# Twenty short streams of unread float32r matmuls, their two sides at other distances in SBUF, between the memory stage and layer 0 of an encoder trunk

## The chip, the cores and the metric

The kernel runs on one core of a Trainium2 chip. The metric is the device time of one launch, in microseconds (us), lower being better. A core has five engines with queues of their own: TensorE (matrix products, PE in the profile; its weight loads have a row of their own, PEld), VectorE (DVE), ScalarE (ACT), GpSimd (POOL) and SyncE (SP, which issues most of the DMAs).

## The reference

Two layers of a bidirectional encoder. `x` and the memory `mem` are 256 x 2048 float32. Each layer projects the normalised `x` onto 7,168 columns, which three head groups share, and projects their joined outputs back onto 2,048 columns.

```python
for l in range(DEPTH):                                   # DEPTH = 2
    h = rmsnorm(x, norm_g[l])
    proj = h @ w_in[l]                                   # 2048 x 7168
    a_x, a_b, a_c, a_g, d_q, d_k, d_v, d_g, m_q, m_g = jnp.split(proj, offsets, axis=-1)
    y_a = short_gated_conv(a_x, a_b, a_c, conv_w[l], conv_b[l]) * jax.nn.silu(a_g)
    ...                                                  # q, k = rmsnorm(d_q), rmsnorm(d_k); lam from lambda_*
    o_d = diff_attention(q, k, v, lam, slopes)           # softmax 1 minus lam times softmax 2, with ALiBi
    y_d = rmsnorm(o_d, diff_head_norm_g[l]) * (1.0 - lam_init) * jax.nn.silu(d_g)
    mkv = rmsnorm(mem, mem_norm_g[l]) @ w_mem_kv[l]      # 2048 x 1024
    ...                                                  # mk, mv, mq from mkv and m_q
    y_m = memory_attention(mq, mk, mv) * jax.nn.silu(m_g)
    x = x + jnp.concatenate([y_a, y_d, y_m], axis=-1) @ w_out[l]   # 2048 x 2048
```

## The kernel before, in words

**Products in three passes.** Every large product is made of float32r matmuls. Each operand is held as a rounded part `hi` and a remainder `lo`; `block` computes hi·hi, hi·lo and lo·hi for each 128 rows of the contraction and each of the two row tiles of `x` (the three lines of `products`, L320, L321 and L322 in the profile). The stationary side is a 128 x 128 piece of the transposed activations, the moving side a 128 x 512 piece of the weights. The activations lie in tiles of the pool `big` (`memT` for the memory, `xT` for the layer's input, `yT` for its output), of the shape [128, 2, 16, 256]: part (hi or lo), contraction tile, row. The pool has two buffers, so `yT` of layer 0 takes the one that `memT` leaves.

**Weights.** `load_w` loads two contraction tiles of 512 columns by DMA into `raw` (four buffers); ScalarE rounds them into `hi` (L294), VectorE subtracts to get `lo` (L295). `hi` and `lo` have four buffers each, so these two engines may run four loads ahead of TensorE and then wait for it.

**Stages.** The memory stage comes first: `memT` is built from `mem` by transposes, and keys and values of the memory are computed for both layers (two blocks of products for each layer). Layer 0 follows with 14 blocks of the input projection, the attention scores and their products in between, and four blocks of the output projection; then layer 1, the same.

**Order.** The tile framework schedules all instructions by a simulated time line, save those that are wrapped in `tc.keep_in_program_order`; these keep the order in which they are written among themselves. Before the change the matmuls of `warm`, small transposes and a number of instructions on ScalarE, VectorE and the DMA queues are wrapped so; the products of `block` are not. Score matmuls write to the pool `ps_s` (tag "s"), two PSUM banks; `block` accumulates in `ps_acc`, four banks.

Of the kernel before, what the change touches and what calls it, by code (L numbers as in the profile page):

```python
# [10 lines left out]
F32 = mybir.dt.float32  # L11
# [7 lines left out]
P = 128  # L19
# [13 lines left out]
NB = 512  # L33
# [14 lines left out]
def encoder(ctx: ExitStack, tc: tile.TileContext, x, mem, norm_g, w_in, conv_w, conv_b,  # L48
            dq_g, dk_g, lq1, lk1, lq2, lk2, head_g, mem_norm_g, w_mem_kv, mq_g, mk_g, w_out, out):
    nc = tc.nc  # L50
    x, mem, out = x[0], mem[0], out[0]

    def pool(name, bufs, space=None):
        kw = {"space": space} if space is not None else {}
        return ctx.enter_context(tc.tile_pool(name=name, bufs=bufs, **kw))
# [9 lines left out]
    ps_s = pool("ps_s", 2, PSUM)  # L65
# [4 lines left out]
    def nm(s):  # L70
        uid[0] += 1
        return f"{s}_{uid[0]}"
# [59 lines left out]
    def g_mnorm(l, k):  # L132
        return cva[:, l * KT + k:l * KT + k + 1]
# [74 lines left out]
    def later(g, n):  # L208
        due[id(g)] = chunk[0] + n
        return g  # L210
# [167 lines left out]
    def col(st, which, t):  # L378
        return st[:, which, t:t + 1]
# [23 lines left out]
    def normed(acc, gs, st, home):  # L403
        return normed_steps(nc.vector, acc, gs, st, home)
# [13 lines left out]
    def sheets(tag):  # L418
        return lambda: sheet(tmp if tag == "e" else keep, tag)
# [257 lines left out]
    def stats_of(parts, tag):  # L677
        ss = small.tile([P, NT], F32, tag="ssum", name=nm("ssum"))
        nc.vector.tensor_reduce(ss, parts, AX.X, ALU.add)
        return row_stats(ss, tag)  # L680

    def T_tile(what):
        kept.append(big.tile([P, 2, KT, SEQ], F32R, tag="T", name=nm(what)))
        return kept[-1]
# [9 lines left out]
    memT = T_tile("memT")  # L694
# [59 lines left out]
    def keys(l, nat):  # L754


        d = dram.tile([NA, B, NA, W_MEM // P * NT * B], F32, name=nm("kd"))
        flat = nat.rearrange("p b j t c -> p b (j t c)")
        for a in range(NA):
            tc.keep_in_program_order(nc.gpsimd.dma_start(d[:, :, a].rearrange("b c r -> c b r"), flat[a * B:(a + 1) * B]))  # L760
        tc.keep_in_program_order(nc.gpsimd.dma_start(flat, d.rearrange("b c a r -> (b c) a r")))
        yield 8
        tc.keep_in_program_order(nc.vector.transpose(
            mkT[l].rearrange("p j (t a i) -> p (j t) a i", t=NT, a=NA),
            nat.rearrange("p a j t c -> p (j t) a c")))
        yield
        tc.keep_in_program_order(nc.scalar.activation(mkT[l], mkT[l], AF.Copy, scale=mgain[:, l:l + 1]))
# [14 lines left out]
    for l in range(DEPTH):  # L782
        if l == 0:
            xT = T_tile("xT")
        mkT.append(keep.tile([P, MH, SEQ], F32, tag=f"mkT{l}", name=f"mkT{l}"))

        mv.append(keep.tile([P, NT, W_MEM], F32, tag="mv" if l == 0 else "bgx", name=f"mv{l}"))
        gm = lambda k: g_mnorm(l, k)
        pinned[0] = l == 0
        acc_k = block(memT, w_mem_kv[l], [(0, NB)], ALLK, gain=gm, before=mem_piece if l == 0 else x_load)  # L790
        if l == 0:
            kraw = keep.tile([P, NT, NB], F32, tag="ga", name="kraw")
            stm.append(keep.tile([P, 6, NT], F32, tag="stm", name="stm"))
        if l > 0:
            tasks.append(later(keys(l, normed(acc_k, P, stm[0], sheets("mqT"))), 10))
        acc = block(memT, w_mem_kv[l], [(W_MEM, NB)], ALLK, gain=gm, before=mem_norm if l == 0 else x_squares)
        pinned[0] = False
        acc_v.append(acc)
        if l > 0:
            for t in range(NT):  # L800
                nc.scalar.activation(mv[l][:, t, :], acc[t], AF.Copy, scale=col(stm[0], R, t))
            away.append(dram.tile([P, NT, W_MEM], F32, name=nm("mvd")))
            nc.sync.dma_start(away[-1], mv[l])
    for l in range(DEPTH):
        st = stats_of(ssx, "st")
        if l > 0:
# [16 lines left out]
        for b in order:  # L823
# [7 lines left out]
            if b == 4:  # L831
                start = chunk[0]
# [119 lines left out]
        for b in range(4):  # L952
# [3 lines left out]
            for t in range(NT):  # L956
                n = 256 if final else NB
# [41 lines left out]
```

## Time and profile before

| what | value |
|---|---|
| time, median of 2 runs | 929.75 us (929.09 and 930.41) |
| span of the profiled execution, first to last instruction | 926.6 us |
| matmul instructions | 4,170, each with a weight load |
| TensorE busy | 919.1 us (99%) |
| VectorE, ScalarE, GpSimd busy | 670.3, 498.7, 16.3 us |
| granted TensorE clock | 0.999 |
| DMA traffic | 215.05 MB, mean 232 GB/s |

The profile gives the span of the profiled execution; its own launch time is not listed apart from it. The median of the runs is 929.75 - 926.6 = 3.15 us longer than the span, which is what lies ahead of the first and behind the last instruction, give or take the spread of the runs. A matmul's row gives its start and its duration; matmuls are pipelined, so that the next one starts before the last has ended, and what one costs is the distance from start to start.

### The profile page before, as it was taken

How to read it: one execution, taken by the hardware profiler on the slowest of the kernel's cores; microseconds unless marked ns; L12 is line 12 of the kernel's file. 1: busy time of each engine (PE TensorE's matmuls, PEld its weight loads, DVE VectorE, ACT ScalarE, POOL GpSimd, SP SyncE). 2: the span in 40 equal slices, each digit the busy share in tenths (PEclk: the TensorE clock that was granted, in tenths of full speed). 3: DMA queues.
4: the chain of work that ended last, by engine and by line, in shares of the span. 5: the costliest groups of instructions: out<-in, count | busy, mean ns of one | idle time of the engine just before them, and what ended most of it. 6: DMA issues, size and time to landing. Idle time of an engine off the chain costs nothing.

```text
span 926.6 us, 12301 instructions
## 1 busy us (share of the span) xinstructions
PE 919.1 (99%) x4170; PEld 760.8 (82%) x4170; DVE 670.3 (72%) x1206; ACT 498.7 (54%) x779; POOL 16.3 (2%) x34
## 2 busy tenths in 40 slices
PE   9999999999999999999999999999999999999998
PEld 6878788888888888888888888888888888888886
DVE  5679788858798786467667757878898777558652
ACT  6758555575555554435455544568554554445431
POOL 0202100000000000000000000000000000000000
PEclk9999999999999999999999999999999999999999
DMA  7897868776669988978587766885889889988662
GB/s 251 251 306 242 304 216 236 234 224 193 191 205 240 254 258 233 269 244 256 205 270 246 235 197 213 246 232 175 249 228 226 258 214 253 252 235 240 210 218 74
DMA packets 251138, 215.05 MB, mean 232 GB/s; under 512 B 131182, under 2 KB 174020, under 8 KB 251076
## 3 DMA queue, kind: packets, MB, share of 16 engines
q1 hardware_dynamic: 248292, 208.76, 76.4%
q0 software_dynamic: 1440, 4.20, 1.6%
q10 hardware_dynamic: 1344, 1.33, 0.5%
q8 instruction: 32, 0.52, 0.2%
q14 instruction: 30, 0.25, 0.1%
HBM read 193.26 MB, written 20.97 MB: 231 GB/s over the span
## 4 chain that ended last, share of the span: by engine, by line
PE 90%; DVE 4%; ACT 3%; DMA 2%; issue 1%; ACTq 0%; DVEq 0%
PE acc L321 29%; PE acc L322 29%; PE acc L320 29%; DMA raw<-in_w_mem_kv_dram 2%; DVE lo L299 2%; PE po L470 2%; ACT hi L298 2%; DVE xf L662 1%; PE s L623 1%; PE s L578 1%; PE s L577 1%; ACT msq L716 0%; DVE xT L267 0%; DVE memT L264 0%; ACT memT L263 0%
## 5 line engine op out<-in xcount | busy, mean ns | idle before, releaser
L294 ACT CAST hi<-raw 128x1024 fp32r<-128x1024 f32 x288 | 302.7, 1052 | 349.8 <-PE acc L322 288.2
L295 DVE TENSOR_TENSOR lo<-raw,hi 128x1024 fp32r<-128x1024 f32 x288 | 351.8, 1223 | 188.4 <-ACT hi L294 178.4
L320 PE MATMUL acc<-hi,xT 128*128 128x512 f32 x896 | 350.5, 393 | 0.0
L322 PE MATMUL acc<-hi,xT 128*128 128x512 f32 x896 | 349.0, 390 | 0.0
L321 PE MATMUL acc<-lo,xT 128*128 128x512 f32 x896 | 348.9, 389 | 0.0
L322 PEld LDWEIGHTS acc<-hi,xT 128*128 128x128 f32 x896 | 168.2, 188 | 35.3
L321 PEld LDWEIGHTS acc<-lo,xT 128*128 128x128 f32 x896 | 168.4, 188 | 33.9
L320 PEld LDWEIGHTS acc<-hi,xT 128*128 128x128 f32 x896 | 168.2, 188 | 33.9
L320 PE MATMUL acc<-hi,yT 128*128 128x512 f32 x256 | 99.6, 389 | 0.0
L321 PE MATMUL acc<-lo,yT 128*128 128x512 f32 x256 | 99.6, 389 | 0.0
L322 PE MATMUL acc<-hi,yT 128*128 128x512 f32 x256 | 99.6, 389 | 0.0
L320 PEld LDWEIGHTS acc<-hi,yT 128*128 128x128 f32 x256 | 48.1, 188 | 10.0
L321 PEld LDWEIGHTS acc<-lo,yT 128*128 128x128 f32 x256 | 48.1, 188 | 10.0
L322 PEld LDWEIGHTS acc<-hi,yT 128*128 128x128 f32 x256 | 48.1, 188 | 9.8
L299 DVE SCALAR_TENSOR_TENSOR lo<-raw,cva,hi 128x512 fp32r<-128x512 f32 x64 | 45.7, 748 | 12.9 <-ACT hi L298 12.9
L321 PE MATMUL acc<-lo,memT 128*128 128x512 f32 x124 | 48.9, 394 | 1.4 <-DVE lo L299 1.4
L298 ACT ACTIVATE hi<-raw,cva 128x512 fp32r<-128x512 f32 x64 | 42.3, 714 | 13.7 <-DMA raw<-in_w_mem_kv_dram 12.3
L322 PE MATMUL acc<-hi,memT 128*128 128x512 f32 x124 | 48.4, 390 | 0.0
L320 PE MATMUL acc<-hi,memT 128*128 128x512 f32 x124 | 44.6, 394 | 0.0
L321 PEld LDWEIGHTS acc<-lo,memT 128*128 128x128 f32 x124 | 23.3, 188 | 8.3 <-DVE lo L299 3.5
L322 PEld LDWEIGHTS acc<-hi,memT 128*128 128x128 f32 x124 | 23.3, 188 | 4.7
L320 PEld LDWEIGHTS acc<-hi,memT 128*128 128x128 f32 x124 | 22.8, 188 | 4.5
(156 smaller groups left out, 643.9 us busy)
## 6 DMA issues: line engine op xcount, KB each, us to landing
raw<-in_w_in_dram SPq DMA_DIRECT2D x192, 512.0 KB, 4.2
raw<-in_w_out_dram SPq DMA_DIRECT2D x64, 512.0 KB, 4.2
raw<-in_w_in_dram SPq DMA_DIRECT2D x64, 256.0 KB, 4.5
raw<-in_w_mem_kv_dram SPq DMA_DIRECT2D x31, 512.0 KB, 6.1
d<-sh SPq DMA_DIRECT2D x80, 128.0 KB, 3.7
sh<-d SPq DMA_DIRECT2D x64, 128.0 KB, 4.6
d<-yn SPq DMA_DIRECT2D x40, 64.0 KB, 4.1
yn<-d SPq DMA_DIRECT2D x40, 64.0 KB, 4.3
```

What stands on the lines that cost most here:

```text
L294: nc.scalar.copy(hi, raw)
L295: nc.vector.tensor_tensor(lo_, raw, hi.bitcast(F32), ALU.subtract)
L298: in_order(nc.scalar.activation(hi[:, j], raw[:, j], AF.Copy, scale=gains_of(j)), nc.vector.scalar_tensor_tensor(lo_[:, j], raw[:, j], gai ...
L299: nc.vector.scalar_tensor_tensor(lo_[:, j], raw[:, j], gains_of(j), hi[:, j].bitcast(F32), ALU.mult, ALU.subtract))
L320: nc.tensor.matmul(acc[t], sh, hi, start=first, stop=False)
L321: nc.tensor.matmul(acc[t], sh, lo, start=False, stop=False)
L322: nc.tensor.matmul(acc[t], sl, hi, start=False, stop=last)
L470: nc.tensor.matmul(po[:, t, :], eT[:, i, t, k, :], v[:, k, h * P:(h + 1) * P], start=k == 0, stop=k == NT - 1)
L577: nc.tensor.matmul(s[c][:, i, :], qi, k_first(yT, c, h), start=True, stop=False)
L578: nc.tensor.matmul(s[c][:, i, :], qi, k_second(yT, k2, c, h), start=False, stop=True)
L623: nc.tensor.matmul(s[:, i, :], qT[:, h, i * P:(i + 1) * P], kT[:, h, :], start=True, stop=True)
L662: tc.keep_in_program_order(nc.vector.transpose(whole.rearrange("p j (n i) -> p j n i", i=B), st.rearrange("p n (c j) -> p j n c", j=QT)))
```

## The change

Behind the memory stage's loop and ahead of the layers' loop, a function `streams` is defined and called once. It takes the two halves of `memT`: `one` (the hi part) gives the stationary side, 128 columns, `two` (the lo part, 16,384 bytes further on in each partition) the moving side, 512 columns. There are 20 streams of 10 matmuls each. In 15 of them the moving side starts 0, 4, 8, 16, 24, 32, 40, 48, 56, 64, 72, 80, 96, 112 or 120 elements of 4 bytes further on; in four the stationary side starts 16, 32, 64 or 96 elements further on; the last has no shift, as the first. All ten matmuls of a stream have the same two sides and accumulate in one bank of `ps_s`, the pool's two buffers taking turns. Nothing reads these banks. The matmuls keep their written order.

```diff
+    def streams():
+
+        one, two = memT[:, 0], memT[:, 1]
+        flat = one.rearrange("p k s -> p (k s)")
+        mov = two.rearrange("p k s -> p (k s)")
+        shapes = []
+        for shift in (0, 4, 8, 16, 24, 32, 40, 48, 56, 64, 72, 80, 96, 112, 120):
+            shapes.append((flat[:, 0:P], mov[:, shift:shift + 512]))
+        for shift in (16, 32, 64, 96):
+            shapes.append((flat[:, shift:shift + P], mov[:, 0:512]))
+        shapes.append((flat[:, 0:P], mov[:, 0:512]))
+        for lhs, rhs in shapes:
+            pw = ps_s.tile([P, NB], F32, tag="s", name=nm("stream"))
...
+            o = pw[:, 0:n]
...
+            for i in range(10):
+                tc.keep_in_program_order(nc.tensor.matmul(o, lhs, rhs, start=i == 0, stop=i == 9))
+
+    streams()
     for l in range(DEPTH):
         st = stats_of(ssx, "st")
```

The lines of the layers move down by 24 (the products of `block` keep theirs). On TensorE's queue the streams stand in ten pairs. In these rows, `acc_870` and `acc_871` are the last accumulators of the memory stage, `acc_1105` and `acc_1106` (after the change `acc_1325` and `acc_1326`) the first block of layer 0. Before, at the end of the memory stage:

```order
L322 MATMUL acc_870<-hi_1057,memT_119 128x512
L320 MATMUL acc_871<-hi_1057,memT_119 128x512
L321 MATMUL acc_871<-lo_1058,memT_119 128x512
L322 MATMUL acc_871<-hi_1057,memT_119 128x512
L321 MATMUL acc_1105<-lo_1110,xT_121 128x512
L322 MATMUL acc_1105<-hi_1109,xT_121 128x512
```

And now, at the same place:

```order
L322 MATMUL acc_870<-hi_1057,memT_119 128x512
L320 MATMUL acc_871<-hi_1057,memT_119 128x512
L321 MATMUL acc_871<-lo_1058,memT_119 128x512
L322 MATMUL acc_871<-hi_1057,memT_119 128x512
L825 MATMUL stream_1079<-memT_119 128x512 x10
L825 MATMUL stream_1090<-memT_119 128x512 x10
L321 MATMUL acc_1325<-lo_1330,xT_121 128x512
L322 MATMUL acc_1325<-hi_1329,xT_121 128x512
```

Two streams, 20 matmuls, have come between the last product of the memory stage and the products of layer 0. A little further on, in the first block of layer 0, with the semaphores that a row waits for (DVE, Activation and PE stand for VectorE, ScalarE and TensorE itself):

```order
L321 MATMUL acc_1326<-lo_1330,xT_121 128x512
L825 MATMUL stream_1101<-memT_119 128x512 [waits PE_49]
L825 MATMUL stream_1101<-memT_119 128x512 x9
L825 MATMUL stream_1112<-memT_119 128x512 [waits PE_49]
L825 MATMUL stream_1112<-memT_119 128x512 x9
L322 MATMUL acc_1326<-hi_1329,xT_121 128x512
L320 MATMUL acc_1325<-hi_1347,xT_121 128x512 [waits Activation_49]
L321 MATMUL acc_1325<-lo_1348,xT_121 128x512 [waits DVE_49]
L322 MATMUL acc_1325<-hi_1347,xT_121 128x512
L320 MATMUL acc_1326<-hi_1347,xT_121 128x512
L321 MATMUL acc_1326<-lo_1348,xT_121 128x512
L322 MATMUL acc_1326<-hi_1347,xT_121 128x512
```

The second pair stands behind nine products of the block, and from the third stream on the first matmul of each waits for the stream that had its bank before, two streams earlier. The other eight pairs follow in the same manner, each nine products behind the last; the last pair is 13 products ahead of the block's end. Apart from these 200 matmuls, all five engines have the same instructions in the same order as before, and all tiles the same addresses.

More of the change, by code (lines that the diff above doesn't have):

```diff
@@ L803, in encoder @@
             nc.sync.dma_start(away[-1], mv[l])
+    def streams():
[10 more added lines that the diff above has]
+            pw = ps_s.tile([P, NB], F32, tag="s", name=nm("stream"))
+            n = 1
+            for d in rhs.shape[1:]:
+                n *= d
+            o = pw[:, 0:n]
+            if len(rhs.shape) == 3:
+                o = o.rearrange("p (a b) -> p a b", b=rhs.shape[2])
+            for i in range(10):
+                tc.keep_in_program_order(nc.tensor.matmul(o, lhs, rhs, start=i == 0, stop=i == 9))
+    streams()
     for l in range(DEPTH):
```

## The prediction

> **What bounds the kernel now.** First I look at the clock and at the busy times by stage, cut at 102 us, where the memory stage ends and where the first streams would stand, and behind it at two stretches of layer 0. Columns: stretch; its length; busy time and count of TensorE's matmuls, of its weight loads, of VectorE, ScalarE and GpSimd; granted clock; DMA share; GB/s.
>
> ```profile
> core 0: 926.6 us, clock 0.999
> 0.00:102.00 102.00, 98.48 (x428) 77.03 (x429) 77.89 (x175) 71.53 (x143) 15.72 (x33) 1.00 0.84 260
> 102.00:926.00 824.00, 820.60 (x3744) 683.74 (x3742) 592.40 (x1032) 427.14 (x637) 0.57 (x1) 1.00 0.78 229
> 102.00:150.00 48.00, 48.00 (x214) 39.75 (x213) 35.31 (x63) 23.92 (x26) 0.57 (x1) 1.00 0.81 262
> 150.00:210.00 60.00, 60.00 (x267) 49.69 (x266) 44.17 (x64) 39.31 (x45) 0.00 (x0) 1.00 0.79 230
> ```
>
> From 102 us to the end TensorE is without a matmul in flight for only 824.00 - 820.60 = 3.4 us, and between 102 and 210 us for none. A busy matmul row alone doesn't prove a bound, since a waiting matmul could count as busy; so the waits come next: who waited for whom, total us, times, longest.
>
> ```profile
> ACT hi L294 <- PE acc L322: 288.2, 186, 3.0
> DVE lo L295 <- ACT hi L294: 178.4, 177, 4.1
> PE acc L321 <- DVE lo L299: 1.4, 4, 0.9
> PE warm L121 <- DVE zeros L116: 1.2, 1, 1.2
> PE pt L646 <- DMA xs<-in_mem_dram: 0.8, 1, 0.8
> ```
>
> ScalarE, which makes `hi` of the weights, waits 288 us for TensorE to give a buffer back, and VectorE behind it. TensorE's own waits are three rows with 3.4 us together, all of the memory stage (L299 works on its weights, L121 and L646 on its start). So the loads run ahead of TensorE in layer 0, and TensorE's issue of matmuls sets the pace. The end of the span holds what little idle time there is:
>
> ```profile
> 922.21 0.39 PE L322 MATMUL acc<-hi,yT 128*128 128x512 f32 x1
> 922.64 0.76 DVE L960 TENSOR_TENSOR xs<-acc,xs 128x256 f32<-128x256 f32 x2 [1.96 <-PE acc L322]
> ```
>
> The last matmul starts at 922.21 and the span ends at 926.6: the last evacuation and its stores, 926.6 - 922.6 = 4.0 us, follow TensorE whatever happens ahead of it. There is no pause in TensorE's queue behind 102 us that 45 us of work could fill.
>
> **The pace of a matmul.** Two rows of the time line of layer 0's first block, 46 matmuls apart (start, duration):
>
> ```profile
> 102.07 0.39 PE L321 MATMUL acc<-lo,xT 128*128 128x512 f32 x1
> ...
> 112.49 0.39 PE L320 MATMUL acc<-hi,xT 128*128 128x512 f32 x1
> ```
>
> (112.49 - 102.07) / 46 = 0.2265 us from start to start. The 0.39 us of a row is latency, most of it beside its neighbours. The streams' matmuls have this very shape and type, 128*128 on the stationary side, 512 columns of float32r on the moving one.
>
> **The change part by part.** *Added:* 20 x 10 = 200 matmuls with their weight loads. That the same weights stand ten times in a row won't save loads: L320 and L321 also use the same weights one behind the other, and the page counts as many weight loads as matmuls (4,170 each). At 0.2265 us, 200 cost 45.3 us.
>
> *Beside what it lies:* nothing on TensorE, whose queue is in order and has no pause there. What lies ahead of the streams doesn't get shorter, what is behind them comes later by their whole length. VectorE and ScalarE have the same instructions in the same order; they make their four loads and then wait for TensorE a little longer. No DMA, no evacuation and no wait of another engine is added.
>
> *The added waits:* 18 of the 20 streams open with a wait for TensorE's own semaphore, on the stream that had the bank before. Queued behind each are the stream's ten matmuls and then the block's products. Between the two stand at least one whole stream and nine products, 19 x 0.2265 = 4.3 us, ten times the latency of 0.39 us, so the wait is over when it is reached. The start of the kernel has the same wait much closer: the third and the fourth of its four `warm` matmuls wait for the first and the second.
>
> ```profile
> 1.20 1.89 PE L121 MATMUL warm<-zeros 128*128 128x512 bf16 x4 [1.20 <-DVE zeros L116]
> ```
>
> Four in 1.89 us, with a last one of about 0.63 us (the mean of L121 is 631 ns), are three steps of 0.42 us, all alike: no pause. I take zero. If the cover were gone, each wait would cost a latency, 18 x 0.39 = 7 us.
>
> *Later users of the two kinds of buffer:* the streams hold `memT`'s buffer, which `yT` of layer 0 takes over, and the two banks of `ps_s`. The first write into `yT` starts at 154.4 us, behind the first block's norm and turn; the last stream stands 13 products ahead of that block's end, so it is done first. The first scores that take the banks start at 210.9 us. Both come later with TensorE's queue, and neither is a new wait: zero.
>
> ```profile
> L502 ACT CAST yT<-sh x4: 616/832/1048, 154.4 to 179.1; 64x1024 fp32r<-64x1024 f32 x2, 64x512 fp32r<-64x512 f32 x2
> L577 PE MATMUL s<-yT x10: 277/283/283, 210.9 to 239.8; 128*128 128x256 f32 x10
> ```
>
> *The distances.* This is the unknown. In the built program `memT`, `xT`, `hi` and `lo` stand at 36,160, 68,928, 118,080 and 134,464 bytes of a partition, and pieces of them at multiples of 512 bytes from there: every 512-wide float32r pair measured above is a multiple of 512 bytes apart, as the unshifted streams are. The other 18 streams are 16 to 480 bytes off that, and no row of before shows such a pair. The nearest rows show that the pace can move by some per cent. The scores (256 columns of float32r, half the work) and the products behind them:
>
> ```profile
> 213.05 0.39 PE L322 MATMUL acc<-hi,xT 128*128 128x512 f32 x1
> 213.27 0.28 PE L578 MATMUL s<-yT 128*128 128x256 f32 x1
> 213.39 0.28 PE L577 MATMUL s<-yT 128*128 128x256 f32 x1
> ...
> 213.99 0.28 PE L578 MATMUL s<-yT 128*128 128x256 f32 x1
> 214.10 0.40 PE L320 MATMUL acc<-hi,xT 128*128 128x512 f32 x1
> 214.34 0.40 PE L321 MATMUL acc<-lo,xT 128*128 128x512 f32 x1
> 214.57 0.39 PE L322 MATMUL acc<-hi,xT 128*128 128x512 f32 x1
> ```
>
> From 213.39 to 213.99 five steps take 0.60 us, 0.120 each, where half of 0.2265 would be 0.113; behind them a product of the usual shape steps 0.24 and the next 0.23. After any such break it takes a few matmuls to fall back to 0.2265. So the weight load, which runs beside the matmul ahead of it, can cost that matmul something, and by how much depends on how the two meet. In the other direction:
>
> ```profile
> 310.72 0.86 PE s L623 x4
> ```
>
> Four plain float32 instructions of the memory scores take 0.86 us in the chain of work, 0.215 each (256 columns an instruction): the nearest step on the other side. The bounds for a shifted stream are so 0.215 (43.0 us for 200) and 0.24 (48.0 us). I take 0.2265, the row with the same shape, type and operand tile, for the whole; 20 breaks of the pace, where the streams and the products meet, might add some 20 ns each, 0.4 us, which stays in the range.
>
> SBUF is described on the Trainium skill's page "SBUF — State Buffer", section "Who interferes with whom", as giving TensorE two independent read ports, so that it never waits on anyone; by that all 20 streams would be alike, 45.3 us. The step of 0.120 beside 0.113 above speaks against that as the whole story.
>
> **Sum.** 929.75 + 45.3 = 975.0 us; in the profile, a span of 926.6 + 45.3 = 971.9 us, with the same 3.15 us around it.
>
> **The rivals.**
>
> *Some distances cost.* If the shifted streams run at up to 0.24, the 180 matmuls in them add 180 x 0.0135 = 2.4 us: 977.5, and 978 with the breaks. For it: the 0.120 above. Against it: the pace found its way back to 0.2265 within a few matmuls in each of those places, and a stream has ten.
>
> *Some distances cost the cover of the weight load.* Where a weight load can't run beside the matmul ahead of it, a step is longer. The memory stage has this once, where `lo` was late:
>
> ```profile
> 99.67 0.50 PE L321 MATMUL acc<-lo,memT 128*128 128x512 f32 x1
> 100.00 0.40 PE L322 MATMUL acc<-hi,memT 128*128 128x512 f32 x1
> ```
>
> 0.33 us for a step. For all 180 shifted matmuls that is 180 x 0.105 = 19 us, 994; for a quarter of the distances 5 us, 980. Nothing in the trace shows this in a settled stream.
>
> *Some distances save.* If the shifted streams fall to 0.215, 180 x 0.0115 = 2.1 us less: 972.9. For it: the plain float32 step of the same length in columns; against: its weight loads and passes are others.
>
> The Trainium skill's page "TensorE: Matmul & The Clock Gate", section "Wait — 56ns, not 53.3ns?", gives 215.7 ns from start to start for 512 columns at full clock; 200 of these would be 43.1 us, an estimate from that page. The 46 steps above, at a granted clock of 0.999, are 11 ns longer, and only the memory scores, plain float32, come near it.
>
> *Not slower: TensorE's pauses take the streams.* If TensorE waited in layer 0 for its weights, the streams would fill those waits, and the loads would get ahead meanwhile. The point from which it decides is 2%, 18.6 us of added time: of 45.3 us the pauses behind 102 us would have to take 26.7. They hold 3.4 us, nearly all behind the last matmul, so this gives 971.6 at the least.
>
> *The streams don't run.* What nobody reads could be left out on the way to the chip: 929.75. Against it: they stand in the built queue in their places, with their waits.
>
> **How the numbers follow.** The forecast, the streams at 0.2265 give or take 0.006 (974 to 976.4), has 0.60. Distances that cost up to 0.24 (976.4 to 978.6): 0.16. Lost cover (over 978.6): 0.07. Distances that save (972.5 to 974): 0.14. Pauses that take the streams: 0.01. Streams that don't run: 0.02. The range from 972.5 to 978.6 takes in the forecast and the first and the third of the rivals, 0.90 by these cases; I don't narrow it, since its ends are the bounds of the unknown step. A measurement of this kernel can tell about 2% from no change; slower by more than that has 0.97, within 2% 0.025, faster 0.005.
>
> **What the changed profile would show.** 4,370 matmuls and as many weight loads; TensorE at 99% of a span near 972 us; each stream's ten matmuls 2.27 us from its first start to the start of what follows; the first write to `yT` near 200 us; ScalarE's wait for L322 or the streams longer by some 40 us, and no new row of more than a microsecond among TensorE's waits. Wrong would be: a stream whose steps differ from 0.2265 by over 0.01 (then the distance counts, and which shift it is tells how), a pause ahead of a stream's first matmul (the wait on the bank), or a span that grows by less than 43 us (something hid the streams).

## The result, and the profile after

The changed kernel takes 977.43 us (977.17 and 977.70) against 929.75: ratio 1.0515, 95% interval 1.0485 to 1.0546, slower by 47.7 us. The range held it, 2.4 us above the forecast.

Clock and busy times of the changed kernel, in the stages ahead of, with and behind the streams, in the columns of before:

```profile
core 0: 975.3 us, clock 1.000
0.00:104.00 104.00, 99.03 (x427) 76.01 (x428) 77.58 (x175) 71.05 (x143) 15.67 (x33) 1.00 0.85 254
104.00:173.00 69.00, 69.00 (x301) 56.24 (x300) 16.20 (x26) 12.93 (x16) 0.56 (x1) 1.00 0.31 103
173.00:975.00 802.00, 798.37 (x3645) 665.15 (x3644) 576.83 (x1007) 414.86 (x623) 0.00 (x0) 1.00 0.80 226
```

TensorE has no gap while the streams run, and as little behind them as before. VectorE and ScalarE are busy for 16 and 13 of those 69 us and the DMA engines for a third: they wait for TensorE. The waits and the streams' own group (busy, mean ns of one, idle time ahead) say the same:

```profile
ACT hi L294 <- PE acc L322: 328.9, 188, 10.9
DVE lo L295 <- ACT hi L294: 230.5, 190, 10.7
L825 PE MATMUL stream<-memT 128*128 128x512 f32 x200 | 48.0, 394 | 0.0
```

ScalarE waits 328.9 - 288.2 = 40.7 us longer for its buffers. No stream waited for anything; but one of its matmuls lasts 394 ns where the products' mostly last 389 or 390. The time line shows what the pairs cost, as the distance from a pair's start to the start of the row behind it (start, duration):

```profile
104.35 4.75 PE L825 MATMUL stream<-memT 128*128 128x512 f32 x20
108.93 0.39 PE L321 MATMUL acc<-lo,xT 128*128 128x512 f32 x1
...
117.67 4.84 PE L825 MATMUL stream<-memT 128*128 128x512 f32 x20
122.34 0.39 PE L322 MATMUL acc<-hi,xT 128*128 128x512 f32 x1
...
164.59 4.78 PE L825 MATMUL stream<-memT 128*128 128x512 f32 x20
169.20 0.39 PE L322 MATMUL acc<-hi,xT 128*128 128x512 f32 x1
```

The first pair (shifts 0 and 4) takes 4.58 us, the third (24 and 32) 4.67, the last (stationary shift 96, and 0) 4.61; at 0.2265 each would be 4.53. All ten pairs add up to 46.35 us, 0.2318 a matmul, 1.0 us over the sum. The block's products between the pairs cost another 0.15 us: worked out from the starts of single records, a few behind most pairs step at 0.228 to 0.237 before they are back at 0.2267. So the streams explain 46.5 us.

What lies behind them only moved: from the end of that block to the last matmul, every matmul starts 48.77 us later than before. So do the first writes into `yT` and the first scores, which take over the two kinds of buffer:

```profile
L502 ACT CAST yT<-sh x4: 611/832/1049, 203.2 to 227.8; 64x1024 fp32r<-64x1024 f32 x2, 64x512 fp32r<-64x512 f32 x2
L577 PE MATMUL s<-yT x16: 278/283/283, 259.6 to 295.5; 128*128 128x256 f32 x16
```

154.4 + 48.8 = 203.2, 210.9 + 48.7 = 259.6. The remaining 48.77 - 46.5 = 2.3 us lie ahead of the first stream, which starts at 104.35; before, the product of layer 0 in this place started at 102.07. The instructions there are the same in the same order. In the experiments with streams below, with the same instructions ahead, the first stream starts between 102.01 and 103.74 us, so this is the spread of the memory stage from run to run; the profile of before was a quick one (span 926.6, where later runs of that kernel had 926.0 to 929.2). In the launch times, 1.2 us of the 47.7 are left beside the 46.5; they are put down to the same spread.

### The profile page after: what moved, and what is told of

Read it like the earlier page. It is cut to its first block, busy times and chain, and to the rows that moved or that the text cites. A ratio compares the mean times of both kernels' runs of the same rounds, so it can differ in the third digit from the quotient of the medians.

```text
span 975.3 us, 12701 instructions
## 1 busy us (share of the span) xinstructions
PE 966.4 (99%) x4370; PEld 797.4 (82%) x4370; DVE 670.6 (69%) x1206; ACT 498.9 (51%) x779; POOL 16.2 (2%) x34
## 4 chain that ended last, share of the span: by engine, by line
PE 90%; DVE 4%; DMA 3%; ACT 2%; issue 1%; SPq 0%; ACTq 0%; DVEq 0%
PE acc L322 27%; PE acc L321 27%; PE acc L320 27%; PE stream L825 5%; DMA raw<-in_w_mem_kv_dram 3%; DVE lo L299 2%; PE po L470 2%; ACT hi L298 1%; DVE xf L662 1%; PE s L623 1%; PE s L578 1%; PE s L577 1%; ACT msq L716 0%; DVE xT L267 0%; ACT memT L263 0%
## 5 line engine op out<-in xcount | busy, mean ns | idle before, releaser
L294 ACT CAST hi<-raw 128x1024 fp32r<-128x1024 f32 x288 | 302.8, 1052 | 394.7 <-PE acc L322 328.9
L825 PE MATMUL stream<-memT 128*128 128x512 f32 x200 | 48.0, 394 | 0.0
L825 PEld LDWEIGHTS stream<-memT 128*128 128x128 f32 x200 | 37.6, 188 | 8.7
```

What stands on the lines that cost most here:

```text
L294: nc.scalar.copy(hi, raw)
L825: tc.keep_in_program_order(nc.tensor.matmul(o, lhs, rhs, start=i == 0, stop=i == 9))
```

## The experiments

Three theories. **A**: what costs is the distance between a matmul's two sides in SBUF, taken modulo 256 bytes (64 elements). **B**: where the moving side starts. **C**: the breaks and the waits on the banks, whatever the operands. In all kernels below but the bfloat16 one, the other instructions stand in the same order as before. The granted clock is 0.999 or 1.000 in every run, so that single steps can be compared. Both sides shifted, fewer columns, the two maps and bfloat16 were run once each and are read from their traces. Where streams have letters, a to t are the 20 in their order.

The change itself already speaks against B: the moving sides of the last pair above both start at the tile's boundary, and it takes 4.61 us. By the unrounded starts, the streams with the stationary side alone moved by 16, 32 and 96 elements take 2.328, 2.336 and 2.336 us, as much as those with a moved moving side, and 64 elements 2.279.

**No shift.**

```diff
-        for shift in (0, 4, 8, 16, 24, ...
+        shapes = [(flat[:, 0:P], mov[:, 0:512])] * 20
```

> All 20 streams without a shift, 200 matmuls as in the change. Theory A (what costs is the distance of the two sides in SBUF): every stream falls back to 0.2265 a matmul, a pair of streams 4.53 to 4.56 us, 45.3 to 45.5 us in all, about 1 us less than the change's 46.35. Theory B (what costs is where the moving side starts): the same, since it starts at the tile's boundary everywhere. Theory C (what costs is the breaks between streams and products and the waits on the two banks, whatever the operands): 46.35 us again, about 4.64 a pair.

Measured: 974.95 us, ratio 1.0477 (1.0459 to 1.0495). The time line, first and last pair:

```profile
103.46 4.70 PE L820 MATMUL stream<-memT 128*128 128x512 f32 x20
108.00 0.39 PE L321 MATMUL acc<-lo,xT 128*128 128x512 f32 x1
...
162.62 4.70 PE L820 MATMUL stream<-memT 128*128 128x512 f32 x20
167.16 0.39 PE L322 MATMUL acc<-hi,xT 128*128 128x512 f32 x1
```

4.54 us a pair, to the last; all 200 take 45.33 us, and the products between them only 0.01 us more than their pace. This is the prediction's sum, with the runs of before beside it: 929.62 + 45.3 = 974.9. That it fits to 0.03 us is luck, as the four runs lie between 971.65 and 975.16; the streams' own time is the evidence. The waits on the banks are all there and cost nothing: C falls.

**The slowest moving shift everywhere.**

```diff
-        for shift in (0, 4, 8, 16, 24, ...
+        shapes = [(flat[:, 0:P], mov[:, 24:536])] * 20
```

> All 20 streams with the moving side 24 elements (96 bytes) further on, the slowest of the change's moving shifts (2.346 us a stream). A and B: 46.8 to 47.1 us in all, some 4.69 a pair, 1.5 us more than without shifts. C: 46.35 us, as in the change.

Measured: 976.66 us, ratio 1.0497 (1.0477 to 1.0518).

```profile
103.74 4.84 PE L820 MATMUL stream<-memT 128*128 128x512 f32 x20
108.41 0.39 PE L321 MATMUL acc<-lo,xT 128*128 128x512 f32 x1
```

4.67 us, and so for all ten pairs: 46.77 us for the 200, and 0.3 us in the products between. The same instructions with the same waits, 1.44 us dearer through 96 bytes. (The whole times' intervals overlap; the streams' own times decide it.) A little under what was expected: the first stream of each pair takes 2.346 us and the second 2.332, with the same operands.

**Both sides shifted alike.** Their distance stays that of no shift.

```diff
+        for shift in (0, 4, 8, 16, 24, 32, 40, 48, 56, 64, 72, 80, 96, 112, 120, 16, 32, 64, 96, 0):
+            shapes.append((flat[:, shift:shift + P], mov[:, shift:shift + 512]))
```

> Both sides shifted alike, by the change's 15 moving and 4 stationary shifts, so that their distance is always the unshifted one, 16,384 bytes, while both start off the boundary. The streams have a letter each in their names. A: 2.27 to 2.28 us a stream, 45.3 to 45.6 in all. B: the shifted streams cost what they cost in the change, 2.28 to 2.35, 46.3 in all.

Measured: 45.84 us in all, between A's 45.3 to 45.6 and B's 46.3. Streams m and n start 96 and 112 elements on:

```profile
143.09 2.43 PE L822 MATMUL stream_m<-memT 128*128 128x512 f32 x10
145.36 2.47 PE L822 MATMUL stream_n<-memT 128*128 128x512 f32 x10
147.66 0.39 PE L322 MATMUL acc<-hi,xT 128*128 128x512 f32 x1
```

2.27 and 2.31 us (2.270 and 2.308 by the unrounded starts), where these moving shifts alone took 2.325 and 2.328 in the change. By the single starts, 15 of the 20 come to steps of 0.226 and 0.227 within their ten matmuls, four more (shifts 24, 40, 112 and the second 16) seem to be still on the way when they end, and only b (4 elements) stays at 0.229 to 0.231. So the distance is most of it, and the 0.2 to 0.5 us above what A expected is the way to the settled pace. All 20 streams have the products' distance between their two sides; what differs is where both start, compared with the matmul ahead. A stream that starts elsewhere than its forerunner seems to enter that way anew, which no run tests by itself. B falls, since shifted moving sides do settle; so does its variant that each side has to start on a boundary of its own, since m settles with both sides 96 elements off it.

**Fewer stationary columns.**

```diff
+        for m in (128, 96, 64, 32):
+            for shift in (0, 16, 24, 32, 64):
+                shapes.append((flat[:, 0:m], mov[:, shift:shift + 512]))
```

> Stationary sides of 128, 96, 64 and 32 columns (streams a to e, f to j, k to o, p to t), each with moving shifts of 0, 16, 24, 32 and 64 elements. A, if the collision is with the reads of the weight load, whose length goes by its columns: the surcharge of shifts 16, 24 and 32 over the unshifted (0.002, 0.007, 0.007 us a matmul at 128 columns) shrinks towards a quarter at 32 columns, and if the step of 0.2265 itself holds such reads beyond 512 columns, the unshifted step falls by up to 0.010. B: the surcharge stays whatever the columns, and the step stays at 0.2265.

Neither. Unshifted streams a (128 columns) and p (32):

```profile
102.91 2.43 PE L823 MATMUL stream_a<-memT 128*128 128x512 f32 x10
105.18 2.47 PE L823 MATMUL stream_b<-memT 128*128 128x512 f32 x10
...
151.97 2.48 PE L823 MATMUL stream_p<-memT 128*32 128x512 f32 x10
154.28 0.40 PE L322 MATMUL acc<-hi,xT 128*128 128x512 f32 x1
```

2.27 us with 128 columns, 2.32 with 32 (2.317 by the unrounded starts), and no stream of fewer than 128 columns settles at 0.2267 at any shift (2.28 to 2.33 us). What shrinks is the spread between the shifts, from 2.27 to 2.35 us with 128 columns to 2.31 to 2.32 with 32, as the cheap distances are gone. The weight load itself does get shorter, 188 ns with 128 columns and 108 with 32, but that doesn't pay; nothing here shows that the step of 0.2267 holds reads that get fewer with the columns.

**A finer map, 30 matmuls a stream.** Theory D says that only the break at a stream's start costs. Here, and in the next map, the 20 streams stand one behind the other with no products between.

```diff
+        for shift in (1, 2, 4, 6, 8, 12, 16, 20, 24, 28, 32, 36, 40, 44, 48, 52, 56, 60, 64, 128):
...
-            for i in range(10):
+            for i in range(30):
```

> 20 streams of 30 matmuls, moving side alone shifted by 1, 2, 4, 6, 8, 12, 16, 20, 24, 28, 32, 36, 40, 44, 48, 52, 56, 60, 64 and 128 elements (streams a to t). Theory A (distance modulo 256 bytes): t and s at the unshifted 0.2267 once settled (about 6.80 us for 30), g (16 elements) about 0.2285, the others between 0.229 and 0.236 for as long as they run (6.9 to 7.05 us for 30), so the surcharge lasts and does not belong to the break at a stream's start. Theory D (only the break costs; each stream falls back to 0.2267 if it is long enough): all 20 streams at 6.80 to 6.87 us. The whole: A about 139 us, D about 136.5.

```profile
103.47 7.26 PE L822 MATMUL stream_a<-memT 128*128 128x512 f32 x30
110.57 7.16 PE L822 MATMUL stream_b<-memT 128*128 128x512 f32 x30
...
145.51 7.16 PE L822 MATMUL stream_g<-memT 128*128 128x512 f32 x30
152.51 7.10 PE L822 MATMUL stream_h<-memT 128*128 128x512 f32 x30
...
222.33 6.97 PE L822 MATMUL stream_r<-memT 128*128 128x512 f32 x30
229.14 7.00 PE L822 MATMUL stream_s<-memT 128*128 128x512 f32 x30
235.98 6.96 PE L822 MATMUL stream_t<-memT 128*128 128x512 f32 x30
242.78 0.39 PE L321 MATMUL acc<-lo,xT 128*128 128x512 f32 x1
```

139.3 us in all, A's number. s and t (64 and 128 elements) take 6.84 and 6.80 us, a (1 element) 7.10, and all others but r over 6.92: the surcharge lasts, so D falls. Two streams don't fit A: g (16 elements) takes 7.00, 0.2333 a matmul, where the change has 0.2285 for the same shift, and r (60 elements) settles at 0.2267.

**The edge of the period.**

```diff
+        for shift in (50, 53, 54, 55, 57, 58, 59, 60, 61, 62, 63, 64, 65, 66, 68, 124, 126, 188, 252, 32):
```

> 20 streams of 20 matmuls, moving side shifted by 50, 53, 54, 55, 57, 58, 59, 60, 61, 62, 63, 64, 65, 66, 68, 124, 126, 188, 252 and 32 elements (streams a to t). Theory A with what the fine map added (60 and 64 settle at 0.2267, 56 at 0.2335, 1 at 0.2366, 4 at 0.2315): the cheap distances form one window just below a multiple of 64 elements, so 61, 62, 63 and 124, 126, 188, 252 settle at 0.2267 too, while 65, 66 and 68 cost 0.231 to 0.237 as 1, 2 and 4 do. Rival G (only a start on a whole 16 bytes is cheap there): 60, 64, 124, 188 and 252 settle, 61 to 63 and 126 do not.

```profile
134.73 4.89 PE L822 MATMUL stream_h<-memT 128*128 128x512 f32 x20
139.46 4.96 PE L822 MATMUL stream_i<-memT 128*128 128x512 f32 x20
144.25 4.77 PE L822 MATMUL stream_j<-memT 128*128 128x512 f32 x20
148.86 4.71 PE L822 MATMUL stream_k<-memT 128*128 128x512 f32 x20
153.40 4.71 PE L822 MATMUL stream_l<-memT 128*128 128x512 f32 x20
157.95 4.89 PE L822 MATMUL stream_m<-memT 128*128 128x512 f32 x20
...
171.97 4.89 PE L822 MATMUL stream_p<-memT 128*128 128x512 f32 x20
176.69 4.76 PE L822 MATMUL stream_q<-memT 128*128 128x512 f32 x20
181.30 4.83 PE L822 MATMUL stream_r<-memT 128*128 128x512 f32 x20
185.96 4.83 PE L822 MATMUL stream_s<-memT 128*128 128x512 f32 x20
```

Both expectations fail. h is 60 elements, the free shift of the last map, and takes 4.73 us, 0.236 a matmul; 124, 188 and 252 (p, r, s), at the same distance modulo 64, take 0.233 to 0.236. 61 (i) is the dearest of all with 0.240; 63 and 64 (k, l) settle at 0.2267. So A needs a second half: off a multiple of 64 elements a stream falls into one of several steady patterns, and the distance alone doesn't say which; streams of the same distance differ by up to 0.010 us. The stream ahead of 60 elements has 56 in one map and 59 in the other, so the way in may decide it; no run shows that. Every stream of the change and of the two maps at a multiple of 64 elements came to 0.2267 after at most eight matmuls.

**bfloat16, and 256 columns.**

```diff
+        zz = keep.tile([P, 3072], mybir.dt.bfloat16, tag="v", name="zz")
+        nc.vector.memset(zz, 0.25)
+        for shift in (0, 8, 16, 32, 48, 64, 96, 128, 192, 256):
+            shapes.append((zz[:, 0:P], zz[:, shift:shift + 512]))
+        for shift in (0, 8, 16, 24, 32, 48, 64, 96, 128, 0):
+            shapes.append((flat[:, 0:P], mov[:, shift:shift + 256]))
```

> Streams a to j in bfloat16 (a tile of constants; 512 columns, moving shifts of 0, 8, 16, 32, 48, 64, 96, 128, 192 and 256 elements of 2 bytes), k to t in float32r with 256 moving columns and shifts of 0, 8, 16, 24, 32, 48, 64, 96, 128 and 0. The scheduler places them further on in layer 0. If the step of 0.2267 beside 512 / 2.4 GHz = 0.2133 belongs to the float32r form, bfloat16 steps at 0.215 to 0.217 at any shift; if it belongs to any matmul whose weights are loaded beside its forerunner, bfloat16 shows 0.22 or more and the shifts show too. At 256 columns A expects 0.113 or 0.120 without a shift (both stand in the trace of before) and other values with shifts that are no multiple of 64 elements.

Streams c and g have shifts of 16 and 96 elements:

```profile
118.10 2.33 PE L826 MATMUL stream_c<-zz 128*128 128x512 bf16 x10
120.27 2.32 PE L826 MATMUL stream_d<-zz 128*128 128x512 bf16 x10
...
130.94 2.33 PE L826 MATMUL stream_g<-zz 128*128 128x512 bf16 x10
133.11 2.32 PE L826 MATMUL stream_h<-zz 128*128 128x512 bf16 x10
```

Each takes 2.17 us, a first step of 0.226 behind the float32r products and nine settled ones. By the starts of single records, the settled steps of all ten bfloat16 streams are 0.215 or 0.216 us at every shift. In float32r with 256 columns the steps lie between 0.113 and 0.125; the unshifted last stream holds 0.120, a shifted one (p, 48 elements) comes down to 0.113. So both the 0.011 us between 0.2157 and 0.2267 and the dependence on the distance belong to float32r here. (The bfloat16 sides lie in one small tile, 0 to 512 bytes apart, the float32r sides 16,384 bytes and more.)

**The same distance in the kernel's own products.** No streams; an unused tile between the pools moves `raw`, `hi` and `lo`, and what lies behind them, by 96, 64 or 256 bytes against `memT`, `xT` and `yT`, for all 3,840 products of 512 columns. Rival E says that only streams which repeat their operands pay, rival F that moving the buffers at all costs something.

```diff
+    gap = pool("gap", 1)
     wp = pool("wp", 3)
...
+    gap.tile([P, 24], F32, name="gap")
```

with 24, 16 and 64 elements.

> The kernel before, without streams; an unused tile of 96 bytes between the pools moves all weight buffers (raw, hi, lo) and what lies behind them 96 bytes on, while memT, xT and yT stay. All 3,840 products of 512 columns then have their two sides 96 bytes off a multiple of 256 bytes. A: each steps at about 0.2336 in place of 0.2267, as the shift of 24 elements does, 3,840 x 0.007 = 27 us, 956 us (950 to 960). Rival E (the surcharge belongs to streams that repeat the same two operands; products that change theirs settle anyway): 930, no change.

> As the last, with 64 bytes. A: 0.2285 as the shift of 16 elements has, 3,840 x 0.0018 = 7 us, 937 us (934 to 941). Rival E: 930. Were 64 bytes as dear as 96, 956.

> The kernel before with the unused tile at 256 bytes: all weight buffers 256 bytes further on. A: the distance modulo 256 is what it was, every product steps at 0.2267, and the time is that of before, 929 to 931 us. Rival F (moving the buffers at all, or the extra tile, costs what the 96 and 64 byte layouts cost): 936 or more.

Measured: 96 bytes 951.3 us, ratio 1.0235 (1.0220 to 1.0251); 64 bytes 936.39, ratio 1.0066 (1.0043 to 1.0088); 256 bytes 930.01, ratio 1.0008 (0.9999 to 1.0018), each in the range that A gave. Busy times from 102 us on, in that order:

```profile
102.00:1000.00 898.00, 843.35 (x3748) 684.38 (x3746) 594.27 (x1034) 426.88 (x638) 0.57 (x1) 1.00 0.74 210
```

```profile
102.00:1000.00 898.00, 829.55 (x3748) 685.18 (x3746) 594.03 (x1034) 427.94 (x638) 0.57 (x1) 1.00 0.73 210
```

```profile
102.00:1000.00 898.00, 821.29 (x3747) 684.32 (x3745) 593.05 (x1034) 428.67 (x638) 0.57 (x1) 1.00 0.74 210
```

Before, TensorE was busy for 820.60 us there; it is 843.4, 829.6 and 821.3 now, with the other engines' work unchanged. With 96 bytes ScalarE waits for TensorE even longer (306.4 us against 288.2), so the moved weight buffers have not made the loads the limit. From layer 0's first product behind the memory stage to the start of the last matmul it takes 820.15 us with the 256 bytes, as before, 841.94 with 96 and 828.05 with 64. Rivals E and F fall: products that change their operands pay for the distance too, and moving the buffers by a whole period costs nothing. The 96 bytes cost 21.8 us over the layers' 3,456 such products, 6.3 ns each where the streams with that shift had 7.2 (1.44 us over 200); the 64 bytes 7.9 us, 2.3 ns each. (The profiled run with 64 bytes was the slowest of four, which lie between 933.86 and 937.49; by their median it is 6.9 us.)

## Why the prediction was right, and where it was not

**The bound and the place: right.** The whole length of the streams is on the path, nothing behind them gets shorter, no other engine becomes late. The two rivals by which the kernel would not be slower are out: the 200 matmuls ran, and TensorE had no pauses for them.

**The waits, the later users, the breaks: right.** No wait on a bank is seen; `yT` and the banks of `ps_s` are taken 48.8 us later, with all of TensorE's queue, and without a wait. The breaks, allowed 0.4 us, cost 0.15.

**The term "200 at 0.2265": mis-sized.** It holds for unshifted streams (45.33 us measured). The step that failed is the one that took the row with the same shape, type and operand tile for all distances, with 0.60 as its chance; what came is the first rival, "some distances cost", which had 0.16. The 180 shifted matmuls took 46.35 - 4.55 = 41.8 us, 0.2322 each, 0.0057 more than the row, within the bounds of 0.215 and 0.24. The argument against that rival, that the pace always falls back within a few matmuls, came from products that all stand at multiples of 512 bytes; off these it doesn't fall back, with few exceptions, in 20 or 30 matmuls either. The step of 0.120 beside 0.113, quoted there for the rival, is no evidence on the distance: with 256 columns an unshifted stream holds 0.120 too.

**The number and the signs.** By the streams alone the time would be 929.75 + 46.5 = 976.25, inside what the forecast allowed for itself (974 to 976.4); that it came out at 977.43, in the rival's stretch, is put down to the spread ahead of the streams. The range held because it took in that rival. The sign named for a distance that counts, steps over 0.01 off 0.2265, is seen in single steps alone (up to 0.241): no stream of the change is more than 0.0081 off in the mean.

**What lies around the span: mis-sized, without harm.** The profiled run of the changed kernel took 977.17 us for its 975.3, 1.9 us; the 3.15 us came from setting a quick profile against the median of other runs.

**The two pages cited.** The Trainium skill's page "SBUF — State Buffer", section "Who interferes with whom", by which TensorE never waits on anyone, would give the shifted streams the time of the unshifted; 46.77 against 45.33 us for the same 200 matmuls speaks against it for float32r. It doesn't show whether the weight load's read and the moving read are what meet. The 215.7 ns of the Trainium skill's page "TensorE: Matmul & The Clock Gate", section "Wait — 56ns, not 53.3ns?", agree with the bfloat16 streams' steps of 0.215 and 0.216, and not with float32r's 0.2267.

## What to carry to other kernels

A matmul that stands in a saturated TensorE queue costs its whole step, and the step read from the trace holds for the same operands at the same distance only; a row of the same shape and type isn't enough. Where float32r products bound a kernel, keep the addresses of stationary and moving tiles a multiple of 256 bytes apart: here a stray 96 bytes between two pools cost 22 us of 930. None of the three layouts tried was faster than that of before, which had this distance everywhere.

## What was not expected of the hardware

- float32r matmuls of 512 columns, each with its weight load of 128 columns, settle at 0.2267 us from start to start when their sides are a multiple of 256 bytes apart (five of the 20 streams with both sides moved did not within their ten matmuls), and run at 0.2267 to 0.240 otherwise; 61 elements were the dearest.
- The pace isn't fixed by the distance alone: 60 elements gave 0.2267 in one stream and 0.236 in another, 16 elements 0.2285 and 0.2333, each steady to its stream's end. What selects the pattern is open.
- Fewer stationary columns make the step longer, not shorter: 0.2317 us with 32 columns, unshifted.
